# A two-layer decoder trunk on one core: six pairs of k-tiles of the last product in seven block products each

## The chip, the cores and the metric

The kernel runs on one core of a Trainium2 chip. The metric is the device time of one execution in microseconds (us). The engines that matter are TensorE (PE; its weight loads, PEld, run beside the matmuls), VectorE (DVE), ScalarE (ACT), GpSimd (POOL) and SyncE (SP), which issues the weight transfers. Each works through its own queue in order; semaphores tie them together. TensorE writes to PSUM, which has eight banks of 128 x 512 numbers of 32 bits; everything else lies in SBUF.

## The reference

Two decoder layers over 256 tokens of width 1024: the first with differential attention, the second with block-sparse attention (one block here, so causal attention), both with cross attention into a memory of 256 rows, each followed by an MLP. Only the last MLP matters here:

```python
def _sq_relu_mlp(h, w_up, w_down):
    u = jax.nn.relu(h @ w_up)
    return (u * u) @ w_down
...
x = x + _sq_relu_mlp(_rmsnorm(x, b_norm_mlp[j]), b_w_up[j], b_w_down[j])
return _rmsnorm(x, final_norm)
```

All in float32: `u` is 256 x 4096, `w_down` 4096 x 1024.

## The kernel before

**Precision.** A float32 product is made of three matmuls in the type `fp32r`. Each factor is split: a high part `h` is its copy cast to `fp32r` (on ACT), a low part `l` is the factor minus the high part (on DVE). Then a*b is ah*bh + al*bh + ah*bl, summed in a PSUM bank. So every chunk of weights (128 x 1024, 512 KB) takes one transfer into a raw buffer `w` (4 of them, L307), one cast into `wh` (6 of them, L330) and one subtraction into `wl` (6, L332); all of that stands in `chunk`.

**The last MLP** (`mlp_last`). First product, `mlp_up`: 16 blocks of two chunks; each chunk gives 128 columns of u, transposed, in an accumulator bank `acc` (4 banks). ACT and DVE add the bank's two halves into the buffer `u` (L779, L781), then relu with the row's norm factor (L787, DVE), square (L790, ACT), and the split of u into `B` tiles (L791 cast, L793 subtraction), which stay in SBUF as the left factor of the second product.

Second product: the 32 k-tiles of 128, one chunk of `w_down` each. The output 256 x 1024 is four cells of 128 x 512 (row half hf, column half c), one bank of class `t` each. For k-tiles 0 to 25, `mm` issues for each cell the three matmuls (L861) with 128 x 128 of u as the stationary and 128 x 512 of the chunk as the moving operand. The last six k-tiles (`HELD`) are kept in the six `wh`/`wl` buffers and done cell by cell, so that a cell's residual addition (L893), square sums (L895), gain (L903) and final norm run while the next cell is computed; the last cell is done in two halves, the second in a bank `acc`.

**What sets the order.** Nothing is issued as written: `P.add` records each step with its engine, an estimated time, what it reads and writes and a priority (its place, moved ahead by the numbers in `EARLY`), and `Plan.order` makes an order by list scheduling before the kernel is emitted. A step gets its buffer there: the free one with the lowest number. Buffers of class `w`, `wh`, `wl` and `acc` are handed out in the order of their first use.

## Time and profile before

| | us |
|---|---|
| median of 3 runs | 606.75 |
| the runs | 605.34, 606.75, 984.32 |
| the profiled execution | 606.42 |
| its span, first to last instruction | 604.6 |
| TensorE, DVE, ACT busy in the span | 592.3, 438.6, 377.2 |

The run of 984.32 stands alone. Busy time adds up instructions; a matmul's end is modelled, so a busy TensorE can still be waiting inside its pipeline. The chain of work that ended last follows, from the last instruction back, what released each step; the timeline lists instructions in order of time, merged where alike, with the idle time ahead of them and what ended it; the table of stretches gives each engine's busy time and the granted TensorE clock between two times.

### The profile page before, as it was taken

To read this page: it belongs to the slowest core of one execution; us is meant where nothing else is said; L and a number is where in the kernel's file an instruction comes from. 1 tells how busy PE (TensorE), PEld (TensorE's weight loads), DVE (VectorE), ACT (ScalarE), POOL (GpSimd) and SP (SyncE) were. 2 spreads that over 40 slices of the span, in tenths; PEclk is the share of its full clock that TensorE was granted. 3 is DMA by queue.
4 is the path that set the end of the run, shared out by engine and by line. 5 is a ranking of instruction groups with operands and counts; after the bars stand their busy time and mean duration, and the time that the engine had idled before them with its cause. 6 is when DMAs were issued, how large, how long until landed. Compare 5 with 4: busy or idle time off the path is not lost.

```text
span 604.6 us, 9476 instructions
## 1 busy us (share of the span) xinstructions
PE 592.3 (98%) x3430; PEld 505.1 (84%) x3430; DVE 438.6 (73%) x800; ACT 377.2 (62%) x771; POOL 55.6 (9%) x67
## 2 busy tenths in 40 slices
PE   8999999999999999999999999999999999999995
PEld 6778878988888888888888887889888888888884
DVE  6689997689887865656777788876888787544435
ACT  6878787576766654444665776776686666443422
POOL 0031020140000000101001123001300000000002
PEclk9989999999999999999999999999999999999998
DMA  8964733436655555555566435344565555555501
GB/s 317 335 206 149 261 108 107 156 129 206 217 201 181 201 178 197 185 186 194 180 208 237 145 105 171 109 140 147 185 226 178 197 184 194 189 185 198 191 20 69
DMA packets 29999, 108.39 MB, mean 179 GB/s; under 512 B 3328, under 2 KB 3328, under 8 KB 29696
## 3 DMA queue, kind: packets, MB, share of 16 engines
q1 hardware_dynamic: 29664, 107.26, 52.9%
q8 instruction: 27, 0.44, 0.3%
q10 hardware_dynamic: 288, 0.52, 0.2%
q14 instruction: 20, 0.16, 0.1%
HBM read 106.72 MB, written 1.05 MB: 178 GB/s over the span
## 4 chain that ended last, share of the span: by engine, by line
PE 93%; DMA 3%; DVE 2%; ACT 1%; issue 0%; SPq 0%; ACTq 0%
PE acc L805 29%; PE acc L493 19%; PE acc L809 15%; PE t L861 14%; PE acc L759 7%; DMA w<-wall 3%; PE t L580 2%; PE t L618 2%; PE t L675 1%; PE t L551 1%; DVE wl L332 1%; DVE xT L745 0%; ACT wh L330 0%; PE acc L861 0%; PE t L845 0%
## 5 line engine op out<-in xcount | busy, mean ns | idle before, releaser
L332 DVE TENSOR_TENSOR wl<-w,wh 128x512 fp32r<-128x512 f32 (+1 forms) x256 | 245.4, 979 | 116.7 <-ACT wh L330 114.3
L330 ACT CAST wh<-w 128x512 fp32r<-128x512 f32 (+1 forms) x256 | 208.8, 840 | 177.1 <-PE acc L805 90.6
L805 PE MATMUL acc<-xn,wh 128*128 128x512 f32 x512 | 131.3, 396 | 0.5 <-DVE xn L348 0.5
L805 PEld LDWEIGHTS acc<-xn,wh 128*128 128x128 f32 x512 | 91.1, 188 | 18.5 <-DVE xn L348 1.8
L493 PE MATMUL acc<-wh,xn 128*128 128x512 f32 x256 | 86.1, 401 | 0.9 <-ACT xn L346 0.9
L861 PE MATMUL t<-wh,B 128*128 128x512 f32 (+1 forms) x256 | 77.2, 384 | 0.0
L809 PEld LDWEIGHTS acc<-xn,wl 128*128 128x128 f32 x512 | 68.1, 188 | 5.6
L809 PE MATMUL acc<-xn,wl 128*128 128x256 f32 x512 | 69.1, 277 | 0.0
L805 PE MATMUL acc<-B,wh 128*128 128x512 f32 x256 | 64.1, 392 | 0.0
L493 PEld LDWEIGHTS acc<-wh,xn 128*128 128x128 f32 x256 | 48.0, 188 | 12.9 <-issue 1.5
L861 PEld LDWEIGHTS t<-wh,B 128*128 128x128 f32 x256 | 47.7, 188 | 9.5
L805 PEld LDWEIGHTS acc<-B,wh 128*128 128x128 f32 x256 | 46.0, 189 | 8.2
L493 PE MATMUL acc<-wl,xn 128*128 128x512 f32 x128 | 50.4, 394 | 0.1
L759 PE MATMUL acc<-B,wh 128*128 128x256 f32 x256 | 50.5, 289 | 0.0
L861 PE MATMUL t<-wl,B 128*128 128x512 f32 (+1 forms) x128 | 49.2, 384 | 0.0
L759 PEld LDWEIGHTS acc<-B,wh 128*128 128x128 f32 x256 | 41.0, 191 | 1.0 <-issue 0.8
L446 POOL TENSOR_TENSOR sqa<-sqa,sq 128x256 f32<-128x256 f32 x21 | 20.7, 988 | 226.5 <-ACT sq L445 225.9
L809 PEld LDWEIGHTS acc<-B,wl 128*128 128x128 f32 x256 | 34.9, 190 | 2.5
L759 PE MATMUL acc<-B,wl 128*128 128x256 f32 x128 | 36.1, 282 | 0.0
L527 POOL TENSOR_TENSOR ropet<-ropes,consts 128x256 f32<-128x256 f32 (+1 forms) x28 | 25.0, 912 | 120.4 <-ACT ropes L516 98.4
L809 PE MATMUL acc<-B,wl 128*128 128x256 f32 x256 | 35.7, 282 | 0.0
L599 ACT ACTIVATE B<-t,nm 128x128 f32<-128x128 f32 (+1 forms) x64 | 27.0, 441 | 7.6 <-DVE nm L595 5.7
(179 smaller groups left out, 727.1 us busy)
## 6 DMA issues: line engine op xcount, KB each, us to landing
w<-wall SPq DMA_DIRECT2D x191, 512.0 KB, 3.3
w<-memt SPq DMA_DIRECT2D x4, 512.0 KB, 4.8
B<-xnat SPq DMA_DIRECT2D x1, 1024.0 KB, 7.8
B<-mnat SPq DMA_DIRECT2D x1, 1024.0 KB, 8.3
xT<-xa SPq DMA_DIRECT2D x1, 540.0 KB, 3.6
w<-w SPq DMA_DIRECT2D x2, 256.0 KB, 3.6
xT<-xb SPq DMA_DIRECT2D x1, 512.0 KB, 6.3
consts<-consts SPq DMA_DIRECT2D x1, 256.5 KB, 4.4
```

The source lines that it names most:

```text
L330: P.add(("act", t_act(n), lambda sl=sl: nc.scalar.copy(h.t[:, sl], w.t[:, sl])), [(w, x) for x in q], [(h, x) for x in q])
L332: P.add(("dve", t_dve(n), lambda sl=sl: nc.vector.tensor_sub(l.t[:, sl], w.t[:, sl], h.t[:, sl].bitcast(F32))), [(w, x) for x in q] + [(h, ...
L446: P.add(("pool", t_pool(S), lambda: nc.gpsimd.tensor_tensor(self.acc.t, self.acc.t, sq.t, op=OP.add)), [sq, self.acc], [self.acc])
L493: nc.tensor.matmul(pss[hf].t[:, c0:c1], a(k)[:, ts], b.t[:, o + c0:o + c1], start=(k == 0 and i == 0), stop=(k == KT - 1 and i == 2))
L527: nc.gpsimd.tensor_tensor(t.t[:, 0:nh, e:e + 32], zs.t[:, 0:nh, 32 - e:64 - e], b(sin[:, e:e + 32]), op=OP.mult)
L580: nc.tensor.matmul(sp[hd].t[:, c], qk[a].t[r, qb * 128:(qb + 1) * 128], qk[b].t[r, S:S + c.stop - c.start], start=(qb == 0 and i == 0 and ...
L599: nc.scalar.activation(p[hd].t[:, c], sp[hd].t[:, c], AF.Exp, bias=nm[hd][:, qb:qb + 1], accum_out=ss[:, hd, qb:qb + 1])
L618: nc.tensor.transpose(ps.t[:, i * 128:(i + 1) * 128], p.t[:, j * 128:(j + 1) * 128], ident)
L759: nc.tensor.matmul(o, a.t[:, ws], x(k), start=(n == 0 and m % 2 == 0 and i == 0), stop=(n == KT - 1 and i == 2), skip_group_check=True)
L805: nc.tensor.matmul(ps.t, wh.t[:, k * 128:(k + 1) * 128], x(k).rearrange("p a s -> p (a s)"), start=start and k == 0, stop=stop and k == 7, ...
L809: nc.tensor.matmul(ps.t[:, 0:S], wl.t[:, k * 128:(k + 1) * 128], x(k)[:, 0], start=False, stop=stop and k == 7, skip_group_check=True)
L861: nc.tensor.matmul(ps.t[:, c0:c1], a, b.t[:, c * 512 + c0:c * 512 + c1], start=(k == k0 and i == 0), stop=(k == 31 and i == 2), skip_group ...
```

## The change

For the second product, the pairs 1, 3, 5, 7, 9 and 11 of k-tiles (`FAST`; k = 2, 3, 6, 7, and so on to 22, 23) are computed in another way. A pair is a product of 2 x 2 blocks (row halves by k-tiles) with 2 x 2 blocks (k-tiles by column halves): 8 block products. A form of Strassen's algorithm needs 7, each still in three matmuls. With A1, A2 the first row half's blocks and A3, A4 the second's, and B1, B2 / B3, B4 those of the weights:

- sums of u, made in the first product right after the square, on DVE, into tiles that are idle by then (`ppx`, `vb`, `mv`): s0 = A3+A4, s1 = s0-A1, s2 = A1-A3, s3 = A2-s1, four instructions of 128 x 128; later their split into `xn` (ACT cast, DVE subtraction, 128 x 512 each);
- sums of the weights, on DVE into the idle `xT`: t0 = B2-B1, t1 = B4-t0, t2 = B4-B2, t3 = B3-t1, 128 x 512 each;
- four weight tiles to split in place of two: B1 (512 wide), B3 and B4 (1024), t0 and t1 (1024), t2 and t3 (1024); so a fast pair holds four of the six `wh` and `wl` buffers;
- seven products: three go straight into a cell's bank, four into the four `acc` banks, which gather over all six pairs;
- after the last fast pair, `gather` adds the four banks into the residual rows `xs` (one ACT copy, eight DVE additions, 128 x 512 each).

No transfer is added. The rest of the diff renames helpers (`product` in `mm`). The core of it:

```diff
+FAST = (1, 3, 5, 7, 9, 11)
...
+            if b in sums:
+                dst, keys = sums[b]
+
+                def blocks(u=u, dst=dst):
+                    a = [u.t[:, k, hf * 128:hf * 128 + 128] for hf in range(2) for k in range(2)]
+                    s = [dst()[:, i * 128:i * 128 + 128] for i in range(4)]
+                    nc.vector.tensor_add(s[0], a[2], a[3])
+                    nc.vector.tensor_sub(s[1], s[0], a[0])
+                    nc.vector.tensor_sub(s[2], a[0], a[2])
+                    nc.vector.tensor_sub(s[3], a[1], s[1])
+                P.add(("dve", 4 * t_dve(128) + 100, blocks), [u], keys, port=True)
...
+        more = [bank("acc") for _ in range(4)]
...
+        def fast_pair(n, j):
...
+            w = [buf("w", [128, CW]) for _ in range(2)]
+            h = [buf("wh", [128, CW], F32R) for _ in range(4)]
+            l = [buf("wl", [128, CW], F32R) for _ in range(4)]
+            for a in range(2):
+                dma(lambda a=a: w[a].t, wall[i + a], 4 * 128 * CW, w=[(w[a], 0), (w[a], 1)])
...
+            def split(x, src, keys, m=CW):
+                P.add(("act", t_act(m), lambda: nc.scalar.copy(h[x].t[:, :m], src())), keys, [h[x]])
+                P.add(("dve", t_dve(m), lambda: nc.vector.tensor_sub(l[x].t[:, :m], src(), h[x].t[:, :m].bitcast(F32))),
+                      keys + [h[x]], [l[x]], port=True)
...
+            split(0, wb(0, 0), [(w[0], 0)], 512)
+            diff(0, wb(0, 1), wb(0, 0), wk[:2])
+            split(1, lambda: w[1].t, wk[2:])
+            diff(1, wb(1, 1), lambda: t(0), wk[3:] + tk(0))
+            split(2, lambda: t(0, 2), tk(0) + tk(1))
+            diff(2, wb(1, 1), wb(0, 1), [wk[1], wk[3]])
+            diff(3, wb(1, 0), lambda: t(1), [wk[2]] + tk(1))
+            split(3, lambda: t(2, 4), tk(2) + tk(3))
...
+            for ps, a, ak, x, c, last in (
+                    (more[0], u_(2 * j, 0), k0, 0, 0, end), (pss[0, 0], u_(2 * j + 1, 0), k1, 1, 0, False),
+                    (pss[0, 1], s_(3), ks, 1, 1, False), (more[1], s_(0), ks, 2, 0, end),
+                    (more[2], s_(1), ks, 2, 1, end), (more[3], s_(2), ks, 3, 0, end),
+                    (pss[1, 0], u_(2 * j + 1, 1), k1, 3, 1, False)):
+                product(ps, a, wcol(x, c), 0, 512, last, ak + [h[x], l[x]])
+            if end:
+                gather()
...
+            P.add(("act", t_act(512, True), lambda: nc.scalar.copy(vt(), r1.t)), [r1], [v])
+            to((0, 0), lambda: r1.t, r1)
+            add(vt, vt, lambda: r6.t, [v, r6], [v])
+            to((0, 1), vt, v, True)
+            to((0, 1), lambda: r5.t, r5)
+            to((1, 1), lambda: r5.t, r5)
+            add(vt, vt, lambda: r7.t, [v, r7], [v])
+            to((1, 0), vt, v, True)
+            to((1, 1), vt, v, True)
...
         for k in range(32):
+            if k // 2 in FAST:
+                ch.append(None)
+                if k % 2:
+                    fast_pair(FAST.index(k // 2), k // 2)
+                continue
             ch.append(chunk())
```

Up to block 1 of the first product of this MLP all engines' orders are as before. **TensorE, second pair of k-tiles** (k = 2, 3). Before, the chunk of k = 3 (the one of k = 2 looks the same): the four cells' banks `t`, two matmuls with the high weights and one with the low ones each:

```order
L861 MATMUL t_5624<-wh_5562,B_892_4895 128x512 x2
L861 MATMUL t_5624<-wl_5572,B_892_4895 128x512
L861 MATMUL t_5631<-wh_5562,B_892_4895 128x512 x2
L861 MATMUL t_5631<-wl_5572,B_892_4895 128x512
L861 MATMUL t_5635<-wh_5562,B_892_4895 128x512 x2
L861 MATMUL t_5635<-wl_5572,B_892_4895 128x512
L861 MATMUL t_5643<-wh_5562,B_892_4895 128x512 x2
L861 MATMUL t_5643<-wl_5572,B_892_4895 128x512
```

Now, from the second of the seven products on (the first reads `wh_5556` into the bank `acc_5697`):

```order
L892 MATMUL t_5651<-wh_5589,B_892_4895 128x512 x2
L892 MATMUL t_5651<-wl_5600,B_892_4895 128x512
L892 MATMUL t_5658<-wh_5589,xn_67 128x512 x2
L892 MATMUL t_5658<-wl_5600,xn_67 128x512
L892 MATMUL acc_5718<-wh_5616,xn_67 128x512 x2
L892 MATMUL acc_5718<-wl_5626,xn_67 128x512
L892 MATMUL acc_5724<-wh_5616,xn_67 128x512 x2
L892 MATMUL acc_5724<-wl_5626,xn_67 128x512
L892 MATMUL acc_5732<-wh_5644,xn_67 128x512 x2
L892 MATMUL acc_5732<-wl_5656,xn_67 128x512
L892 MATMUL t_5664<-wh_5644,B_892_4895 128x512 x2
L892 MATMUL t_5664<-wl_5656,B_892_4895 128x512
```

Eight groups of three per chunk pair become seven; four of the seven read the split sums in `xn`, four tiles of weights take the place of two, and each engine's order around them goes on pair by pair.

**DVE, middle of the second product.** Before, nothing but the low parts of the chunks, one row each:

```order
L332 TENSOR_TENSOR wl_5802<-w_5738,wh_5797 128x1024
L332 TENSOR_TENSOR wl_5820<-w_5756,wh_5815 128x1024
L332 TENSOR_TENSOR wl_5838<-w_5774,wh_5833 128x1024
L332 TENSOR_TENSOR wl_5856<-w_5792,wh_5851 128x1024
L332 TENSOR_TENSOR wl_5874<-w_5810,wh_5869 128x1024
```

Now, one period of a plain pair (k = 20, 21, L336) and the fast pair behind it (L926 the sums of weights, L916 the low parts):

```order
L926 TENSOR_TENSOR xT_66<-w_5992 128x512
L336 TENSOR_TENSOR wl_6023<-w_5951,wh_6017 128x1024
L926 TENSOR_TENSOR xT_66<-w_6004,xT_66 128x512
L926 TENSOR_TENSOR xT_66<-w_6004,w_5992 128x512
L926 TENSOR_TENSOR xT_66<-w_6004,xT_66 128x512
L336 TENSOR_TENSOR wl_6049<-w_5980,wh_6037 128x1024
L916 TENSOR_TENSOR wl_6056<-w_5992,wh_6044 128x512
L916 TENSOR_TENSOR wl_6063<-w_6004,wh_6054 128x1024
L916 TENSOR_TENSOR wl_6075<-xT_66,wh_6068 128x1024
L916 TENSOR_TENSOR wl_6087<-xT_66,wh_6080 128x1024
```

The four differences stand ahead of the splits that read them, around the plain chunks' splits.

**DVE, end of the second product.** Before, the last two splits around a residual addition:

```order
L332 TENSOR_TENSOR wl_6086<-w_6026,wh_6081 128x1024
L871 TENSOR_TENSOR ql_4728<-ql_4728,t_5643 128x256
L332 TENSOR_TENSOR wl_6103<-w_6044,wh_6097 128x1024
L893 TENSOR_TENSOR qh_4709<-qh_4709,t_5624 128x256 x2
L893 TENSOR_TENSOR qh_4714<-qh_4714,t_5631 128x256 x2
```

Now, the last five splits (k = 27 to 31) among the gathering additions (L972; `qh` and `ql` are the residual rows, `u_6132` the gathered copy):

```order
L336 TENSOR_TENSOR wl_6148<-w_6085,wh_6134 128x1024
L336 TENSOR_TENSOR wl_6158<-w_6111,wh_6146 128x1024
L972 TENSOR_TENSOR u_6132<-u_6132,acc_5724 128x512
L972 TENSOR_TENSOR ql_4728<-ql_4728,acc_5718 128x512
L972 TENSOR_TENSOR qh_4714<-qh_4714,u_6132 128x512
L336 TENSOR_TENSOR wl_6181<-w_6141,wh_6169 128x1024
L336 TENSOR_TENSOR wl_6189<-w_6153,wh_6179 128x1024
L972 TENSOR_TENSOR qh_4714<-qh_4714,acc_5718 128x512
L972 TENSOR_TENSOR u_6132<-u_6132,acc_5732 128x512
L972 TENSOR_TENSOR ql_4719<-ql_4719,u_6132 128x512
L336 TENSOR_TENSOR wl_6208<-w_6163,wh_6198 128x1024
L972 TENSOR_TENSOR ql_4728<-ql_4728,u_6132 128x512
```

The addition `qh_4709<-qh_4709,acc_5697`, the first one that needs a finished bank, and behind it the splits of k = 25 and 26 stand ahead of this piece; the last split now stands behind seven of the eight additions.

## Rows read from the trace of the kernel before

**Rows 1.** The page's head: span, then busy time of each engine.

```profile
span 604.6 us, 9476 instructions
PE 592.3 (98%) x3430; PEld 505.1 (84%) x3430; DVE 438.6 (73%) x800; ACT 377.2 (62%) x771; POOL 55.6 (9%) x67
```

**Rows 2.** The chain that ended last, around the last product: start, length, work.

```profile
507.70 1.86 PE acc L805 x8
509.56 0.91 PE acc L809 x8
510.47 85.13 PE t L861 x384
595.60 2.17 PE acc L861 x18
```

**Rows 3.** Busy time by stretch (count in brackets), clock, DMA share, GB/s.

```profile
core 0: us, PE busy (x) PEld busy (x) DVE busy (x) ACT busy (x) POOL busy (x), PEclk, DMA share, GB/s
440.00:510.30 70.30, 70.30 (x409) 61.30 (x409) 57.18 (x80) 48.29 (x80) 0.00 (x0) 1.00 0.58 194
510.30:597.80 87.50, 87.46 (x404) 72.97 (x402) 40.84 (x53) 32.94 (x45) 5.04 (x7) 1.00 0.45 150
597.80:604.60 6.80, 0.00 (x0) 0.00 (x0) 2.91 (x12) 1.31 (x4) 0.00 (x0) 0.75 0.21 77
```

**Rows 4.** Timeline of TensorE, last product: start, us, line, operation, tiles.

```profile
511.01 0.61 PE L861 MATMUL t<-wh,B 128*128 128x512 f32 x2
...
547.73 0.61 PE L861 MATMUL t<-wh,B 128*128 128x512 f32 x2
```

**Rows 5.** Timeline of VectorE, the last MLP's first product (idle before in brackets).

```profile
432.39 0.48 DVE L471 TENSOR_SCALAR dg<-ident,rstd 128x128 f32<-128x128 f32 x2
...
439.72 1.29 DVE L793 TENSOR_TENSOR B<-u,B 128x512 fp32r<-128x512 f32 x2
...
502.37 1.23 DVE L332 TENSOR_TENSOR wl<-w,wh 128x1024 fp32r<-128x1024 f32 x1 [0.49 <-ACT wh L330]
503.51 0.41 DVE L781 TENSOR_TENSOR u<-u,acc 128x256 f32<-128x256 f32 x1
503.84 0.68 DVE L793 TENSOR_TENSOR B<-u,B 128x512 fp32r<-128x512 f32 x1
```

**Rows 6.** Timeline of ScalarE, end of the first and of the second product.

```profile
506.83 1.06 ACT L330 CAST wh<-w 128x1024 fp32r<-128x1024 f32 x1 [1.45 <-PE acc L805]
507.78 0.63 ACT L790 ACTIVATE u<-u 128x512 f32<-128x512 f32 x1
508.31 0.35 ACT L779 COPY u<-acc 128x256 f32<-128x256 f32 x1
508.56 0.62 ACT L791 CAST B<-u 128x512 fp32r<-128x512 f32 x1
...
581.02 1.05 ACT L330 CAST wh<-w 128x1024 fp32r<-128x1024 f32 x1 [1.67 <-PE t L861]
```

**Rows 7.** Timeline of VectorE, last product: middle and end.

```profile
552.19 1.23 DVE L332 TENSOR_TENSOR wl<-w,wh 128x1024 fp32r<-128x1024 f32 x1 [1.50 <-ACT wh L330]
...
581.25 0.42 DVE L871 TENSOR_TENSOR ql<-ql,t 128x256 f32<-128x256 f32 x1 [0.64 <-PE t L861]
582.11 1.23 DVE L332 TENSOR_TENSOR wl<-w,wh 128x1024 fp32r<-128x1024 f32 x1 [0.44 <-ACT wh L330]
585.33 0.75 DVE L893 TENSOR_TENSOR qh<-qh,t 128x256 f32<-128x256 f32 x2 [2.00 <-PE t L861]
```

**Rows 8.** SP's waits from 505; its DMA issues there; page: GB/s by slice.

```profile
SPq L307 <- DVE wl L332: 51.6, 22, 3.5
...
w<-wall SPq DMA_DIRECT2D x25, 512.0 KB, 3.2
...
GB/s 317 335 206 149 261 108 107 156 129 206 217 201 181 201 178 197 185 186 194 180 208 237 145 105 171 109 140 147 185 226 178 197 184 194 189 185 198 191 20 69
```

More of the change, by code (lines that the diff above doesn't have):

```diff
@@ L252, in part, with ppx_buf @@
         return Buf(cls, lambda slot: parent.t[:, slot, 0:width], parent)
+    def ppx_buf():
+        return Buf("ppa", lambda slot: ppx[:, slot])
     def fixed(shape, nm, dt=F32):
@@ L637, in plain_T @@
         if par is None:
-            pp = [Buf("ppa", lambda slot: ppx[:, slot]) for _ in range(2)]
+            pp = [ppx_buf() for _ in range(2)]
         else:
@@ L766, in out_proj, with mlp_up @@
                 done(m)
-    def mlp_up(st):
+    def mlp_up(st, sums=()):
         st.rstd()
@@ L849, in mlp_last @@
             xs[hf, c] = x
-        us = mlp_up(st)
+        places = [ppx_buf() for _ in range(2)]
+        sums = {}
+        for i, j in enumerate(FAST):
+            if i < 2:
+                sums[j] = (lambda b=places[i]: b.t), [places[i], ("s", j)]
+            elif i < 5:
+                sums[j] = (lambda i=i: vb.rearrange("p a b e -> p (a b e)")[:, (i - 2) * 512:(i - 1) * 512]), [
+                    ("vb", n, hf) for n in range(2) for hf in range(2)] + [("s", j)]
+            else:
+                sums[j] = (lambda: mv.rearrange("p a b e -> p (a b e)")), [("mv", 0), ("mv", 1), ("s", j)]
@@ L851, in mlp_last, with product @@
+        us = mlp_up(st, sums)
         pss = {cell: bank("t") for cell in cells}
+        more = [bank("acc") for _ in range(4)]
         ch = []
-        def mm(k, hf, c, c0=0, c1=512, ps=None, k0=0):
-            wh, wl = ch[k]
-            ps = ps or pss[hf, c]
+        begun = set()
+        def product(ps, a, b, c0, c1, stop, keys):
+            start = ps not in begun
+            begun.add(ps)
             def emit():
-                uh, ul = [us[k // 4].t[:, k % 4, i, hf * 128:(hf + 1) * 128] for i in range(2)]
-                for i, (a, b) in enumerate(((uh, wh), (ul, wh), (uh, wl))):
-                    nc.tensor.matmul(ps.t[:, c0:c1], a, b.t[:, c * 512 + c0:c * 512 + c1],
-                                     start=(k == k0 and i == 0), stop=(k == 31 and i == 2), skip_group_check=True)
-            P.add(("pe", t_mm(c1 - c0, 3), emit), ukeys(us, k) + [(wh, c), (wl, c)], [ps])
+                (ah, al), (bh, bl) = a(), b()
+                for i, (x, y) in enumerate(((ah, bh), (al, bh), (ah, bl))):
+                    nc.tensor.matmul(ps.t[:, c0:c1], x, y, start=start and i == 0, stop=stop and i == 2,
+                                     skip_group_check=True)
+            P.add(("pe", t_mm(c1 - c0, 3), emit), keys, [ps])
@@ new lines, in gather, with add, to @@
+        def gather():
+            v = buf("u", [128, 2, S])
+            vt = lambda: v.t.rearrange("p a s -> p (a s)")
+            def add(dst, a, b, r, w, port=False):
+                P.add(("dve", t_dve(512), lambda: nc.vector.tensor_add(dst(), a(), b())), r, w, port=port)
+            def to(cell, src, key, port=False):
+                x = xs[cell]
+                add(lambda: x.t, lambda: x.t, src, [(x, 0), (x, 1), key], [(x, 0), (x, 1)], port)
+            r1, r5, r6, r7 = more
+            P.add(("act", t_act(512, True), lambda: nc.scalar.copy(vt(), r1.t)), [r1], [v])
[7 more added lines that the diff above has]
+            to((1, 1), vt, v, True)
@@ L883, in mlp_last @@
                         for k in range(held, 32):
-                            mm(k, hf, c, 256 * i, 256 * i + 256, tail if i else None, held if i else 0)
+                            mm(k, hf, c, 256 * i, 256 * i + 256, tail if i else None)
                         ps = tail if i else ps
```

32 lines of the change are left out of this document (added).

## The prediction

> **What bounds the kernel now.** I read the busy shares first, then the chain of waits that ended last, then a table of stretches, then the timelines. TensorE is busy for 592.3 of 604.6 us [rows 1], but a busy share says nothing of who waits for whom; the chain does. In it the whole last product is one piece, 384 matmuls in 85.13 us, followed by 18 more in 2.17 us [rows 2]: nobody releases TensorE there. The stretches agree: from 510.3 to 597.8 TensorE is busy for 87.46 of 87.50 us at a granted clock of 1.00 (the 2.4 GHz level), while VectorE (DVE) works 40.84 and ScalarE (ACT) 32.94 [rows 3]. So in this stage a matmul less is time less, as long as DVE and ACT still deliver. The last 6.8 us hold no TensorE work at all [rows 3] and aren't touched.
>
> **Removed.** A pair of k-tiles has 8 block products of 3 matmuls; a fast pair has 7. Six pairs lose 18 matmuls of 128x512. Their pace: the row at 511.01 and the row at 547.73 are 54 products of three apart [rows 4], so 36.72 us for 162, or 0.2267 each (a matmul's own 0.39 is longer, since they overlap). Removed: 18 x 0.2267 = **4.08 us**. The new products have the same shapes and the same three passes, and each bank change after three matmuls was there before, so I keep the pace.
>
> **Added on DVE and ACT.** Costs are paces, that is, start to next start while the queue is full. DVE: 1024 wide 1.14 (502.37 to 503.51), 256 wide 0.33 (503.51 to 503.84), 512 wide 0.61 (two take 1.29, one alone 0.68) [rows 5]. A tensor subtraction 128 wide isn't in the trace; between 256 and 1024 an element costs 1.05 ns, which gives 0.20; two narrow ones of another kind took 0.48 [rows 5]. I take 0.25, with 0.20 and 0.28 (a lone 256 of 0.41 less 0.13) as ends. ACT: 1024 wide 0.95 (506.83 to 507.78), 512 wide 0.53 (507.78 to 508.31) [rows 6].
>
> *Sums of u in the first product*: four 128 wide steps in six of sixteen blocks, 1.0 us each (0.8 to 1.1). A block takes 5.54 us of TensorE (two chunks of 1.86 + 0.91 [rows 2]); DVE is busy for 57.18 of 70.30 us there [rows 3], so 1.03 us of each block is free, and every second block has no sums. Hidden. What would break it: the accumulator banks are handed out lowest number first, so every second chunk reuses one bank and its eviction has one chunk (2.77 us) to be done; behind a 1.14 us split it ends some 1.1 us ahead. Late next would be the first matmul of the next chunk.
>
> *A fast pair against a plain one.* Plain: two casts and two subtractions, 1024 wide. Fast: casts 512 + 3 x 1024 + 512 (the sums); subtractions 512 + 3 x 1024 + 512; four differences of weights, 512 wide. The order repeats a plain pair and a fast pair, for which TensorE needs 24 + 21 matmuls, 10.20 us. DVE needs 5 x 1.14 + 6 x 0.61 = 9.36, ACT 5 x 0.95 + 2 x 0.53 = 5.81. So DVE goes from half idle (1.50 us before each 1.23 us split [rows 7]) to 92%, and doesn't become the bound. Rate isn't enough; lateness matters too. I laid the DVE rows of the new order on TensorE's clock, each starting at the latest of the row before, its cast, and the TensorE read that frees its buffer. Of the six high and six low tiles a fast pair holds four; each tile replaces the one six tiles earlier (two low tiles swap), so a plain tile may be split 7.5 us before its use (10.20 - 2.72). One period, zero where its plain pair starts on TensorE: the first plain tile's buffer is free at 2.72, the next one there is cast at 3.8 and split at 4.9; three differences to 6.7; second plain split 7.9; fast splits 8.5, 9.6, 11.5 (its low buffer is read until 10.20) and 12.7; the next pair's first difference 13.3; then DVE waits for the next plain cast at 14.0. It is used from 10.20 to 19.0 in this order, so each is there 5 us early. At the start, with zero at the end of the first product, the first fast pair's tiles and sums are ready at -7.0, -4.3, -0.6, 2.2 and 2.8 and are used from 5.44 to 8.84. Its first accumulator bank is free at about 3.2, after the last eviction of the first product, and used at 5.44: 2.2 us to spare. In the second pair the splits of four pairs' sums come on top; there and later 3.8 us or more remain, growing again. Nothing on TensorE waits.
>
> *Weights.* No DMA is added, and SP's order stays. Four transfers of 512 KB per 10.20 us are 206 GB/s; the slices reach 335 [rows 8]. A raw buffer of a fast pair is held longer (until its second difference or split), but was refilled in 3.2 us after release [rows 8] and comes due 4 to 5 us after it. SP already waits on DVE for its buffers (51.6 us over 22 waits [rows 8]), so a late DVE shows there first. Cost nothing.
>
> *Gathering.* One ACT copy and eight 512 wide DVE additions stand between the splits of the last eight chunks. Here the cover is thinnest. On the same clock (five periods of 10.20, a plain pair of 5.44, a product of 0.68) the last fast pair's first product is done at 57.1; DVE waits for it (0.2 for the signal), then works through seven splits and seven additions until the last chunk's low tile: 7 x 1.14 + 7 x 0.61 = 12.25, so it is ready at 69.6. The held products begin at 66.6 (57.1 + 4.08 + 5.44), and the sixth one's third matmul is the first to read it: 66.6 + 5 x 0.68 + 0.45 = 70.5. Spare: **0.9 us**, less some tenths for additions that depend on each other. Before, the same tile was ready at 583.34 (582.11 + 1.23) [rows 7] and needed at 581.03 + 3.85 = 584.88: 1.5 us. Bounds: nothing, or, with lone durations (1.23 and 0.68) in place of paces, 13.4 us and a stall of 0.2 to 0.5. I take nothing. ACT isn't the limit: its last cast began as soon as the buffer was free (581.02 [rows 6]) and takes 1.05.
>
> *A rule against it.* In rows 5 a DVE instruction starts 0.07 to 0.09 us before the end of the one before it. The Trainium skill, "VectorE: DVE Perf Modes", section "The DRAIN you can't avoid", says that the next instruction doesn't start until the pipe is empty; the trace disagrees by that overlap. By that rule DVE would pay lone durations, 5 x 1.23 + 6 x 0.68 = 10.23 per period, as much as TensorE: no rate lost, but no lateness made good. It is the third rival below.
>
> **Sum.** The profiled execution took 606.42 us (span 604.6 and 1.8 around it): 606.42 - 4.08 = 602.3. It lies 0.3 under the median of the runs shown (606.75; the other run near it took 605.34), so I say **602.4**.
>
> **Rivals.**
> 1. *Hidden, as above*: 602.4; with the runs' own spread 601.2 to 603.4. Chance 0.74.
> 2. *The gather makes the last splits late.* Each addition on DVE that costs 0.3 us more than I took delays the last low tile by 2.1 us; stalls of 0.5 to 3 us give 603 to 605.5. For it: 0.9 us is little, and additions that read the accumulators have no 512 wide row. Against: two 256 wide ones from an accumulator took 0.75 [rows 7], as on chip memory. Chance 0.14.
> 3. *DVE pays lone durations* (the rule above): the same late tile, and the second and third fast pairs eat up to 2 us of spare; stalls of 0.5 to 2 us, 603 to 604.5. Chance 0.06.
> 4. *DVE becomes the bound, slower than before.* With x for a 512 wide step the period is 5.70 + 6x and passes 10.20 at x = 0.75. The spare of some 3 us goes first; over the five periods the gain of 4.08 is gone when the excess is (4.08 + 3) / 5 = 1.42 us, x = 0.99. At x = 1.1 the stalls are 5 x (12.30 - 10.20) - 3 = 7.5, which gives 606.42 - 4.08 + 7.5 = 609.8. No row comes near (0.61 to 0.69). Chance 0.05.
> 5. *Nothing changes, because TensorE doesn't get shorter*: a pace of 0.2373 in place of 0.2267 over the 384 matmuls that remain would eat the 4.08, and give 606.4. New waits stand ahead of most products; but plain chunks wait for both engines as well, at this pace. Chance 0.01.
>
> **Range.** The first case alone spans 601.2 to 603.4. Adding the lower part of cases 2 and 3 holds eight in ten: **601.0 to 604.8**. About 2% (12 us) is what a measurement of this kernel can tell from no change. Faster by that would need three times the matmuls removed: 0.01. Slower by that needs 16 us of stalls, x about 1.4 in case 4, or a disturbance I don't see: 0.02. Within: 0.97.
>
> **What would show it.** Of the changed kernel: 402 - 18 = 384 matmuls in the last product, TensorE without idle time from 510 on, its end near 593.7 in place of 597.8, 6.8 us behind it; DVE 85 to 95% busy between 516 and 567; the last low tile split near 580. An idle stretch of TensorE shortly before a matmul of a fast pair would speak for 4, one near 580.5 for 2 or 3. I'm wrong if the matmuls' pace changes, if a bank's eviction holds a chunk of the first product, or if the splits miss their time by more than the spare named.

## The result, and the profile after

Five executions of the changed kernel have a median of 603.47 us (602.59 to 604.52); the kernel before has 606.75 beside them. The ratio is 0.9948, with a 95% interval of 0.9923 to 0.9974: a small gain of about 0.5%, inside the 2% named ahead, 1.1 us over the 602.4 that was forecast and inside its range. The profiled execution took 604.05 us; its page begins like this (columns as in [rows 1]):

```profile
span 602.3 us, 9555 instructions
PE 588.9 (98%) x3412; PEld 502.4 (83%) x3412; DVE 474.4 (79%) x874; ACT 390.8 (65%) x790; POOL 56.0 (9%) x67
```

Against [rows 1] there are 18 matmuls less, 74 instructions more on DVE and 19 more on ACT, which is what the steps of the change add up to. The span is 2.3 us shorter. Where these 2.3 us come from is read from the chain that ended last (start, length, work), the answer to [rows 2]:

```profile
511.63 5.46 PE t L892 x24
...
521.19 6.12 PE t L892 x27
...
531.42 6.12 PE t L892 x27
...
572.33 20.54 PE t L892 x99
592.87 2.17 PE acc L892 x18
```

The last product runs from 511.63 to 595.04, 83.41 us. Before it ran from 510.47 to 597.77, 87.30 us [rows 2]. So the part that was changed is 3.89 us shorter. It began 1.16 us later, though, and 0.43 us more follow behind it (602.3 - 595.04 = 7.26 us, before 604.6 - 597.77 = 6.83): -3.89 + 1.16 + 0.43 = -2.30. Neither is the change's work that was costed. Nearly all of the 0.43 us is a stretch of VectorE ahead of its last 512 wide scaling, in which it waits for nothing that the profile shows (so `issue`; before, it idles 0.1 us there):

```profile
597.80 0.42 issue
```

It stands in the chains of both profiled executions of the change and of the kernel with the gathering behind the splits, and not in those of the other kernels below; with the eighth product and with three pairs 6.87 and 6.91 us follow the last product. So it goes with the kernel and not with the execution; what makes it isn't shown. As to the start, the chains of before and after part in the kernel's first 33 us, at the first weights:

```profile
20.02 7.87 DMA w<-wall
...
32.56 9.83 PE acc L497 x35
```

Before, the same wait took 6.72 us and the same piece of TensorE's work began at 31.74. In the kernels profiled below whose first product isn't held up, the last product begins anywhere from 509.05 to 512.13. One total of one execution therefore can't show 4 us; the length of the stage can.

The stretches (columns as in [rows 3]): the first product, the last one, and the part in which the pairs with 7 products follow one another.

```profile
440.00:510.30 70.30, 70.30 (x405) 61.17 (x405) 63.65 (x108) 48.75 (x81) 0.00 (x0) 1.00 0.58 196
510.30:593.70 83.40, 83.40 (x385) 69.54 (x384) 71.19 (x98) 46.79 (x64) 4.31 (x6) 1.00 0.45 158
516.00:567.00 51.00, 51.00 (x226) 42.12 (x225) 46.08 (x54) 30.28 (x33) 0.00 (x0) 1.00 0.58 203
```

TensorE has no idle time in any of them that the table counts, at a granted clock of 1.00. DVE is busy for 46.08 of 51.00 us in the third, 90%, where 85 to 95% was forecast. In the first product DVE's busy time rose from 57.18 [rows 3] to 63.65 us in 70.30, by the sums of u and by differences that begin early.

VectorE's rows (idle before in brackets): one block's sums of u, a fast pair's differences of weights, the largest wait for a transfer, and the end of the gathering with the last low tile.

```profile
441.47 0.28 DVE L802 TENSOR_TENSOR ppx<-u 128x128 f32<-128x128 f32 x1
441.79 0.29 DVE L803 TENSOR_TENSOR ppx<-ppx,u 128x128 f32<-128x128 f32 x1
442.00 0.28 DVE L804 TENSOR_TENSOR ppx<-u 128x128 f32<-128x128 f32 x1
442.20 0.28 DVE L805 TENSOR_TENSOR ppx<-u,ppx 128x128 f32<-128x128 f32 x1
442.41 0.68 DVE L809 TENSOR_TENSOR B<-u,B 128x512 fp32r<-128x512 f32 x1
...
537.43 0.69 DVE L926 TENSOR_TENSOR xT<-w,xT 128x512 f32<-128x512 f32 x1 [0.44 <-DMA w<-wall]
538.04 0.69 DVE L926 TENSOR_TENSOR xT<-w,w 128x512 f32<-128x512 f32 x1
538.64 0.68 DVE L926 TENSOR_TENSOR xT<-w,xT 128x512 f32<-128x512 f32 x1
...
547.00 0.69 DVE L926 TENSOR_TENSOR xT<-w 128x512 f32<-128x512 f32 x1 [2.51 <-DMA w<-wall]
...
577.66 1.23 DVE L336 TENSOR_TENSOR wl<-w,wh 128x1024 fp32r<-128x1024 f32 x1 [0.56 <-ACT wh L334]
...
578.80 0.68 DVE L972 TENSOR_TENSOR qh<-qh,acc 128x512 f32<-128x512 f32 x1
579.40 0.68 DVE L972 TENSOR_TENSOR u<-u,acc 128x512 f32<-128x512 f32 x1
580.11 0.69 DVE L972 TENSOR_TENSOR ql<-ql,u 128x512 f32<-128x512 f32 x1
580.72 1.22 DVE L336 TENSOR_TENSOR wl<-w,wh 128x1024 fp32r<-128x1024 f32 x1
```

The four sums take 0.94 us (441.47 to 442.41); the differences follow at 0.61 and 0.60 us. The additions that read the accumulators (L972) take 0.68 and are followed 0.60 us later by independent work (578.80 to 579.40), but 0.71 later (579.40 to 580.11) by one that reads what the first wrote. The last low tile ends at 581.94, where a split near 580 was forecast.

TensorE's rows, first inside a pair with 7 products, then where the last low tile is first read:

```profile
548.28 0.61 PE L892 MATMUL t<-wh,B 128*128 128x512 f32 x2
...
548.96 0.62 PE L892 MATMUL t<-wh,xn 128*128 128x512 f32 x2
...
549.65 0.62 PE L892 MATMUL acc<-wh,xn 128*128 128x512 f32 x2
...
581.46 0.39 PE L892 MATMUL t<-wl,B 128*128 128x512 f32 x1
581.68 0.62 PE L892 MATMUL t<-wh,B 128*128 128x512 f32 x2
582.14 0.40 PE L892 MATMUL t<-wl,B 128*128 128x512 f32 x1
582.38 0.63 PE L892 MATMUL t<-wh,B 128*128 128x512 f32 x2
```

A product that reads u directly takes 0.68 us (548.28 to 548.96), one that reads the sums (`xn`) 0.69. The matmul that first reads the last low tile starts at 582.14, in its place, 0.68 behind the one of its kind at 581.46. The load of its stationary factor, which goes ahead of it, doesn't:

```profile
581.23 0.19 PEld L892 LDWEIGHTS t<-wl,B 128*128 128x128 f32 x1
...
581.99 0.19 PEld L892 LDWEIGHTS t<-wl,B 128*128 128x128 f32 x1
```

These loads lie 0.68 us apart, so this one was due at 581.91. It starts 0.05 us behind the split's end at 581.94. In the second profile of the change and in the kernel with raw buffers of their own (below) the same load also starts 0.05 us behind the split, and there the profile names the split as what it waited for (0.16 and 0.31 us). So nothing was left: the tile came 0.08 us late for the load, on which the wait for it sits. TensorE lost 0.02 to 0.03 us by it, since the next product starts 0.70 behind the one before (581.68 to 582.38) instead of 0.68.

SP's waits in the last product (who waits for whom: us in total, times, longest), its transfers of weights with the median time to landing, the answers to [rows 8]:

```profile
SPq L311 <- DVE wl L336: 51.1, 14, 9.0
...
w<-wall SPq DMA_DIRECT2D x26, 512.0 KB, 3.9
```

Before, 51.6 us in 22 waits, none longer than 3.5, and 3.2 us to landing [rows 8]. The total is about the same, but SP now stands for up to 9.0 us before one buffer and then sends several transfers at once, which land later. The other engines' waits in the last product (same columns) show who meets this, and ScalarE's timeline shows one of its waits near the end:

```profile
ACT wh L334 <- PE t L892: 15.7, 11, 1.7
...
DVE xT L926 <- DMA w<-wall: 3.8, 3, 2.5
```

```profile
576.57 1.05 ACT L334 CAST wh<-w 128x1024 fp32r<-128x1024 f32 x1 [1.48 <-DMA w<-wall]
```

### The profile page after: what moved, and what is told of

Same layout as the page of the kernel before. It is cut to its first block, busy times and chain, and to the rows that moved or that the text cites. A ratio compares the mean times of both kernels' runs of the same rounds, so it can differ in the third digit from the quotient of the medians.

```text
span 602.3 us, 9555 instructions
## 1 busy us (share of the span) xinstructions
PE 588.9 (98%) x3412; PEld 502.4 (83%) x3412; DVE 474.4 (79%) x874; ACT 390.8 (65%) x790; POOL 56.0 (9%) x67
## 4 chain that ended last, share of the span: by engine, by line
PE 92%; DMA 3%; DVE 3%; ACT 1%; issue 0%; SPq 0%; DVEq 0%; ACTq 0%
PE acc L821 29%; PE acc L497 19%; PE acc L825 15%; PE t L892 11%; PE acc L763 7%; PE acc L892 3%; DMA w<-wall 2%; PE t L584 2%; PE t L622 2%; PE t L679 1%; DVE wl L336 1%; PE t L555 1%; DMA xT<-xa 1%; DVE xT L749 0%; ACT wh L334 0%
## 5 line engine op out<-in xcount | busy, mean ns | idle before, releaser
L334 ACT CAST wh<-w 128x512 fp32r<-128x512 f32 (+1 forms) x244 | 196.1, 829 | 153.1 <-PE acc L821 85.8
L336 DVE TENSOR_TENSOR wl<-w,wh 128x512 fp32r<-128x512 f32 (+1 forms) x244 | 230.5, 966 | 73.8 <-ACT wh L334 73.1
L892 PE MATMUL t<-wh,B 128*128 128x512 f32 (+1 forms) x184 | 55.2, 382 | 0.0
L892 PEld LDWEIGHTS t<-wh,B 128*128 128x128 f32 x184 | 34.1, 188 | 6.7
L892 PE MATMUL t<-wl,B 128*128 128x512 f32 (+1 forms) x92 | 35.2, 382 | 0.0
```

Of the source, the lines that this page charges most:

```text
L334: P.add(("act", t_act(n), lambda sl=sl: nc.scalar.copy(h.t[:, sl], w.t[:, sl])), [(w, x) for x in q], [(h, x) for x in q])
L336: P.add(("dve", t_dve(n), lambda sl=sl: nc.vector.tensor_sub(l.t[:, sl], w.t[:, sl], h.t[:, sl].bitcast(F32))), [(w, x) for x in q] + [(h, ...
L892: nc.tensor.matmul(ps.t[:, c0:c1], x, y, start=start and i == 0, stop=stop and i == 2, skip_group_check=True)
```

## The experiments

Each kernel's last product is measured in its profile, from its first matmul to the end of its last, and its time beside that of the kernel before on the same chip. The times are medians of 10, 5, 4 and 6 executions for the eighth product, the change, the change again and the seven pairs; the others have one. The kernel before beside them has 5 executions (606.75), 13 (606.54), 1 (604.40) and 11 (607.68). The views below have the columns told above.

| kernel | last product, us | run, us | kernel before beside it, us |
|---|---|---|---|
| before | 87.30 | 606.75 | |
| the change | 83.41 | 603.47 | 606.75 |
| an eighth product | 87.46 | 606.95 | 606.54 |
| three pairs, not six | 85.34 | 604.87 | 606.54 |
| 2 more additions in the gathering | 84.68 | 605.37 | 606.54 |
| 4 more additions | 88.01 | 605.79 | 606.54 |
| differences twice | 96.39 | 617.49 | 604.40 |
| differences three times | 110.79 | 636.92 | 604.40 |
| gathering behind the splits | 83.38 | 602.60 | 604.40 |
| raw buffers of their own | 83.61 | 603.65 | 604.40 |
| the change again | 83.41 | 601.59 | 607.68 |
| seven pairs | 82.63 | 603.43 | 607.68 |
| differences twice, own raw buffers | 92.92 | 613.44 | 607.68 |
| 4 more additions, gathering behind the splits | 83.37 | 605.09 | 607.68 |

### Is it the missing product that saves the time?

Everything of the change stays, and each pair gets an eighth product back.

```diff
-  (more[0], u_(2 * j, 0), k0, 0, 0, end), (pss[0, 0], ...
+  (more[0], u_(2 * j, 0), k0, 0, 0, False), (more[0], u_(2 * j, 0), k0, 0, 0, end), (pss[0, 0], ...
```

> Every fast pair gets an eighth product of three matmuls: the first of the seven is computed twice into its bank (the output counts it double). DVE, ACT and the weights do what they do in the changed kernel. The last product took 87.30 us before (from 510.47 to 597.77) and 83.41 in the changed kernel (511.63 to 595.04). Theory (what was bought is 18 matmuls of TensorE, all that DVE got is hidden): the 18 matmuls come back at 0.227 us each, 83.41 + 4.08 = 87.5 us for the last product, and the time is that of the kernel before within 1 us. Rival (DVE or the raw weights set the pace of the changed kernel by now, and TensorE waits for them unseen): the added matmuls fill waiting time, and the product stays between 83.4 and 86.

Its chain:

```profile
509.07 5.46 PE t L892 x24
...
594.36 2.17 PE acc L892 x18
```

509.07 to 596.53 is 87.46 us, as expected, and the time is the old one (606.95 against 606.54; ratio 1.0003, 0.9978 to 1.0027). All that the change adds costs 0.16 us of this stage. The gain is the 18 matmuls and nothing else.

The second takes half the pairs:

```diff
-FAST = (1, 3, 5, 7, 9, 11)
+FAST = (1, 5, 9)
```

> Only the pairs 1, 5 and 9 are fast. Theory (each fast pair is worth 0.68 us of TensorE less 0.03 for its slightly slower products, and the gathering costs nothing): the last product takes 87.30 - 3 x 0.65 = 85.35 us. Rival (a fixed cost comes with the first fast pair, as the gathering, or a fixed gain with the new order): a loss of some tenths to 1 us against that line, 85.6 to 86.4, or 83.4 already.

Measured 510.85 to 596.19, 85.34 us. The gain goes with the number of products left out: 1.96 us for nine matmuls, 3.89 for eighteen.

### How much was there to spare in the gathering?

Two, then four more additions of 128x512 on DVE, ahead of the last low tile:

```diff
+                for _ in range(2):
+                    nc.vector.tensor_add(ppx[:, 0], vt(), r7.t)
+                nc.vector.tensor_add(vt(), vt(), r7.t)
```

The other kernel has `range(4)`; the last of these lines stood there before.

> Two more additions, 512 wide, into an idle tile, stand on DVE among the gathering ones ahead of the last chunk's split; all else is in the same order. In the changed kernel that split ended at 581.94, and the third matmul of the sixth held product, which reads it first, was due at 578.20 + 5 x 0.68 + 0.45 = 582.05. Theory by that trace (the spare is 0.1 us): 1.22 us more on DVE stall TensorE by 1.1, the last product takes 84.5. Theory of the prediction (spare 0.9): a stall of 0.3, 83.7. Rival (the gathering is off the path by more than either): 83.4.

> As the run with two more additions, but four, 2.44 us of DVE. Spare of 0.1: a stall of 2.3 us, the last product takes 85.8. Spare of 0.9: a stall of 1.5, 84.9. Off the path: 83.4. Between the two runs the stall should grow by 1.22 if the spare is used up in the first.

With two, TensorE waits before the first matmul that reads the last low tile; the chain passes through a late transfer of weights (572.25, 4.42 us), a cast, a split and the additions before it reaches this row:

```profile
583.63 0.50 PE L892 MATMUL t<-wl,B 128*128 128x512 f32 x1 [1.01 <-DVE wl L336]
```

The last product is 84.68 us, 1.27 longer. The chain has the last split ahead of it:

```profile
582.36 1.23 DVE wl L336
```

So the last low tile is ready at 583.59, 71.64 us after the product's start at 511.95, where the change has 70.31 (581.94 - 511.63): 1.33 later. What the tile loses the product loses, but for 0.06, so the change had no spare to speak of; less the forecast 0.9, two additions of 0.7 us would have given 0.5. With four the product is 88.01 us, 4.6 us longer, and its tile is ready 73.44 us after the start (581.26 + 1.23 - 509.05), 3.1 later. The rows show the rest: the wait, and the granted clock (third figure from the end of the stretches; DMA share and GB/s stand behind it).

```profile
582.53 0.80 PE L892 MATMUL t<-wl,B 128*128 128x512 f32 x1 [2.82 <-DVE wl L336]
```

```profile
579.00:582.50 3.50, 0.71 (x4) 0.25 (x2) 3.40 (x6) 0.00 (x0) 0.00 (x0) 0.99 0.00 0
582.50:585.00 2.50, 2.47 (x6) 1.99 (x7) 1.66 (x4) 0.91 (x4) 0.45 (x1) 0.50 0.00 0
585.00:588.00 3.00, 3.00 (x13) 2.45 (x12) 0.00 (x0) 0.00 (x0) 0.97 (x2) 0.86 0.00 0
```

After 2.82 us without work TensorE ran at the 1.2 GHz level (0.50) for some 3 us before it was back at 2.4: the same last 55 matmuls took 12.36 us here and 10.83 in the kernel with two more. That is another 1.5 us, paid behind the wait.

### Does DVE become the bound where the fourth rival says?

Each difference of weights is issued twice, and three times:

```diff
-  ... lambda: nc.vector.tensor_sub(t(a), x(), y())), keys, ...
+  ... lambda: [nc.vector.tensor_sub(t(a), x(), y()) for _ in range(2)]), keys, ...
```

> Each of the four 128x512 differences of a fast pair's weights is issued twice with the same result. DVE's work in a block of 10.23 us of TensorE rises from about 8.75 us, once the sums of xn's tiles are made, by 4 x 0.61 = 2.44 us to 11.2 us. Theory (DVE is a server with 10.23 us per block, and what it does not get done is carried over from block to block until the spare is gone): an excess of about 1.0 us per block over five blocks, less some 3 to 4 us of lead, so the last product is 0 to 2 us longer than the 83.4 us of the change, the run about 604 to 606 us. Rival (DVE's lone durations of 0.69 us are what counts, and its 10% of idle time cannot be used): an excess of 1.3 to 2.3 us per block, the last product 3 to 9 us longer. Second rival (DVE's added work is hidden whatever it is): no change to 83.4 us.

> The same differences are issued three times. Theory: 8.75 + 4.88 = 13.6 us of DVE's work in a block of 10.23 us, an excess of 3.4 us over five blocks and a last one, less 3 to 4 us of lead: the last product 13 us longer than 83.4 us (11 to 17), about 616 us, with TensorE waiting on DVE in every block from the second on. Lone durations: 8.75 + 8 x 0.69 = 14.3 us or more, 16 to 20 us longer. Second rival (hidden whatever it is): 83.4 us again.

Measured: 96.39 us (512.46 to 608.85), 13.0 longer than the change, and 110.79 us (517.40 to 628.19), 27.4 longer. DVE is the bound, as the theory has it, but the price is far beyond every figure expected; the runs are 617.49 and 636.92 us. The doubled kernel's rows, one block of DVE, and TensorE's waits in the last product:

```profile
543.03 1.42 DVE L926 TENSOR_TENSOR xT<-w 128x512 f32<-128x512 f32 x2 [0.71 <-DMA w<-wall]
...
555.43 1.42 DVE L926 TENSOR_TENSOR xT<-w 128x512 f32<-128x512 f32 x2 [0.72 <-DMA w<-wall]
```

```profile
PE t L892 <- DVE wl L336: 8.0, 6, 2.1
```

```profile
594.20:597.20 3.00, 2.97 (x8) 2.33 (x9) 1.66 (x4) 0.91 (x4) 0.95 (x2) 0.62 0.00 0
```

A block is 12.40 us (543.03 to 555.43), not 11.2. Two things were missed. A repeated difference writes the tile that the one before it just wrote, and starts 0.72 us behind it (1.41 less 0.69) instead of 0.61, so four cost 2.9 instead of 2.44: 11.7 us of work. And 0.7 us per block is a wait for a transfer. TensorE's own waits make 8.0 of the 13.0 us. The other 5.0 us are busy time: the same matmuls take 88.40 us in place of 83.40, at a granted clock of 0.62 behind the last wait, for instance. Two stretches make 2.8 of them: ten matmuls behind the wait of 1.85 us took 3.76 us where 2.58 were usual behind a wait, and the last 55 took 12.45 where the kernel with two more additions had 10.83; the rest is spread over the other waits. In the kernel with three, 18.8 us are waits; its first product was held up as well, by 3.6 us.

To part the work from the transfers, the doubled differences were given raw buffers of their own (the edit is shown with the kernel that has only that, below):

> The differences issued twice and, at once, raw buffers of their own for the pairs with 7 products. Theory (of the 13.0 us that the doubled differences cost, DVE's work of 11.6 us per block explains a part, its waits of some 0.7 us per block for transfers that are no longer early another): without these waits the excess is 1.4 instead of 2.1 us per block over five blocks, less 3 us of lead, 4 us of stalls and some 2 us more at the lower clock; last product 87 to 91 us. Rival (DVE waits for transfers only because it is late anyway, and its own work sets the pace): 95 to 97 us, as with shared buffers.

```profile
542.00 1.41 DVE L926 TENSOR_TENSOR xT<-wx 128x512 f32<-128x512 f32 x2
...
553.75 1.41 DVE L926 TENSOR_TENSOR xT<-wx 128x512 f32<-128x512 f32 x2
```

```profile
PE t L892 <- DVE wl L336: 6.2, 5, 2.1
```

```profile
547.26 0.50 PE L892 MATMUL t<-wl,B 128*128 128x512 f32 x1 [1.51 <-DVE wl L336]
...
590.19 0.50 PE L892 MATMUL t<-wl,B 128*128 128x512 f32 x1 [2.09 <-DVE wl L336]
```

The block is 11.75 us, nothing but work, and the last product 92.92 us: 9.5 longer than the change, 3.5 less than with shared buffers. That lies between theory and rival. The waits for transfers were a real part of the price, about a quarter; the work of DVE is the larger one. The theory's own sum, 4 us of stalls in the blocks, came out: the first wait comes only at 547.26, and the three in the blocks make 3.9 us (1.51, 1.18 and 1.22). What it left out stands in front of the products kept for the end, where nothing was spare: 0.22 and 2.09 us. And the matmuls took 3.3 us more of busy time (86.68 against 83.40) where some 2 were expected.

### What holds the last low tile?

Two candidates: the additions that stand ahead of it on DVE, and the weights that come in bursts. First the additions go behind the last split:

```diff
-            if end:
-                gather()
...
-                P.add(("dve", t_dve(512), lambda: nc.vector.tensor_add(dst(), a(), b())), r, w, port=port)
+                P.add(("dve", t_dve(512), lambda: nc.vector.tensor_add(dst(), a(), b())), r + [(ch[31][1], 0)], w,
+                      port=port)
...
+        gather()
```

Each addition now also waits for the last low tile (`ch[31][1]`).

> DVE makes the eight additions of the gathering only behind the last split of the weights instead of among the last splits. Theory (the additions stand ahead of the last low tiles on DVE and use up their spare): the last low tile is ready 2 to 3 us earlier against its need than the 0.1 us of the change, the last product keeps its 83.4 us, and the work behind it, 9.0 us to the end of the span, grows by 0 to 1 us. Rival (the late weights alone set the last low tile, and DVE has nothing to do ahead of it): the spare stays at 0.1 to 0.5 us.

```profile
577.92 1.22 DVE L336 TENSOR_TENSOR wl<-w,wh 128x1024 fp32r<-128x1024 f32 x1 [0.97 <-ACT wh L334]
```

The last low tile is ready at 579.14, 68.94 us after the product's start at 510.20; in the change it was 70.31 (581.94 - 511.63). That is 1.4 us earlier, less than the 2 to 3 expected, since DVE now waits for casts (0.97 in this row). The load ahead of the matmul isn't held any more, and the last product is 83.38 us, 0.03 under the change; 7.22 us follow it, as in the change (7.26, not the 9.0 named ahead).

Then the additions stay and the pairs with 7 products get raw buffers of their own:

```diff
-            ... "p": 4, "z": 4, "v": 2}
+            ... "p": 4, "z": 4, "v": 2, "wx": 2}
...
-            w = [buf("w", [128, CW]) for _ in range(2)]
+            w = [buf("wx", [128, CW]) for _ in range(2)]
...
-                dma(lambda a=a: w[a].t, wall[i + a], 4 * 128 * CW, w=[(w[a], 0), (w[a], 1)])
+                dma(lambda a=a: w[a].t, wall[i + a], 4 * 128 * CW, r=[("x", 0), "rb"], w=[(w[a], 0), (w[a], 1)])
```

The last line also makes these transfers wait for two tiles of this MLP (`xT`, `rb`).

> The raw weights of the fast pairs get two buffers of their own, so that the queue's next transfer does not wait for the split of a plain pair. Theory (the queue stands behind a buffer that comes free late, up to 9.0 us, and then sends four tiles at once, which land in 3.9 us instead of 3.2): DVE's waits on transfers in the last product, 3.8 us in three places, go under 1 us, and the last low tile is ready 0.5 to 1 us before its need instead of 0.1 us; the last product keeps 83.4 us. Rival (the transfers are late because all of them share the chip's memory with others): the landing stays at 3.9 us and DVE's waits at 3 us or more.

DVE's waits for transfers are gone from the list of waits of the last product (3.8 us in three places in the change), but the last low tile didn't come earlier: 581.60, which is 70.51 us after the start. The load ahead of the matmul waits 0.31 us for it, and the last product is 83.61 us. In place of the transfers DVE's splits of plain pairs wait for casts, 5.0 us in five places (1.6 in two in the change). The theory held for the middle of the product and fell for its end. SP still stands up to 9.0 us, the transfers into the buffers of their own land after 4.3 us and the others after 3.2, and two casts at the end still wait for transfers, 1.57 and 1.59 us (1.50 and 1.48 in the change). What holds these last transfers isn't shown. ACT's waits for TensorE to free high tiles (15.7 us, 11 times, in the change) suggest that raw buffers wait for a cast which waits for a high tile; that was not tried, and the kernel before had more of these waits (40.6 us, 25 times) and no late transfers.

Last, both additions and place at once, the four additions behind the last split:

> The four more additions in the gathering, which made TensorE wait 2.8 us, and the gathering behind the last split. Theory (the additions cost only because they stand ahead of the last low tile on DVE): no wait of TensorE, last product 83.4 us, its last low tile 68.9 us after the product's start as without the four. Rival (the late weights hold the last splits, wherever the additions stand): a wait of 1 us or more, 84.5 us or more.

```profile
579.84 1.23 DVE L336 TENSOR_TENSOR wl<-w,wh 128x1024 fp32r<-128x1024 f32 x1 [0.77 <-ACT wh L334]
```

Ready at 581.07, 68.94 us after the start at 512.13, to the hundredth the figure without the four; no wait, 83.37 us of last product. The same four additions that cost 4.6 us ahead of the tile cost TensorE nothing behind it. They do lengthen what follows the product, to 7.8 us.

### The change again, and a seventh pair

```diff
-HELD = 6
-FAST = (1, 3, 5, 7, 9, 11)
+HELD = 4
+FAST = (1, 3, 5, 7, 9, 11, 13)
...
```

The seventh pair's sums of u get a tile of their own, and the gathering is placed as above.

> The change itself once more, beside the seventh pair and on the same chip. Theory: 83.4 us of last product, 3.3 us (0.5%) under the kernel before. Its start of the last product should differ by about 1 us from that of the execution profiled first, since nothing ahead of the last MLP was changed.

> A seventh pair of k-tiles is made with 7 block products, the last four k-tiles stay for the end instead of six, and the gathering stands behind the last split. Theory (a matmul less is time less as long as the splits come in time): three matmuls less, 0.68 us, so the last product takes 82.7 us against 83.4 of the change; about 0.7 us under the change measured beside it. Rival (with only four plain k-tiles behind the last such pair the last splits come late): TensorE waits 1 to 3 us before the products that were kept for the end, the last product takes 84 to 87 us, and the run is 0.5 to 3 us over the change.

The change has 83.41 us of last product again, from 510.50 on, and its last low tile is ready 70.35 us after that. Its ratio is 0.9900 here (0.9879 to 0.9921; 601.59 against 607.68) and was 0.9948 (0.9923 to 0.9974) the first time. The intervals don't overlap, with the same stage to the hundredth: the rest of the program, or the chip, moves the totals by more than the intervals say. Of the 6.1 us of the second measurement the stage explains 3.9.

Seven pairs have 82.63 us of last product, 0.78 less, a little more than the three matmuls' 0.68, and TensorE waits nowhere in it; the rival fell. But 7.69 us follow instead of 7.29, and the time is 603.43 us (600.18 to 604.82; ratio 0.9930, 0.9907 to 0.9953), which isn't under the change's 601.59. It is no better version as measured; the 0.4 us that its profile leaves are too small for these runs.

## Why the prediction was right

**Removed: right, but for 0.19 us.** 4.08 us were forecast for 18 matmuls at 0.2267, and the last product lost 3.89. The eighth product put back gives the time back, and half the pairs give half.

**The pace kept: off by 0.03 us a pair.** A plain and a fast pair take 10.23 us (521.19 to 531.42 in the chain of after), not 10.20, and six times 0.03 is nearly all of the 0.19 missing; where the last low tile isn't late (83.38 us, the gathering behind the splits) 0.16 is missing. The rows place it at the products that read the sums, 0.69 apart instead of 0.68. With the eighth product the stage is 0.16 over before, so it comes with the form and not with the count. The text had taken equal shapes for equal pace; why reading from that tile is slower isn't settled.

**Sums of u: right.** 0.94 us where 1.0 was taken (0.8 to 1.1), hidden: TensorE is busy all through the first product. The narrow subtraction that the trace of before didn't show takes 0.28; the next starts 0.20 to 0.21 behind it, or 0.32 where it reads what the one before wrote (441.47 to 441.79). 0.25 was taken, 0.20 and 0.28 were the ends.

**DVE and ACT in a block: right.** 0.60 to 0.61 us for a difference, the same for an addition from the accumulators where nothing depends on the one before, and 90% busy. So the third rival fell: DVE pays paces. By the Trainium skill, "VectorE: DVE Perf Modes", section "The DRAIN you can't avoid", each of these would start only when the one before had left the pipe; the trace disagrees for independent ones (0.60 after a 0.68), and is close to it for one that reads or overwrites what the one before wrote (0.71 and 0.72). The same section of the Trainium skill lets a next instruction that isn't held start earlier (what holds one stands in "Two Vector instructions with no wait between them"), an exception that the prediction left out; the rows of independent ones agree with that. The fourth rival's mechanism exists, and its price was set too low: it counted only the excess of work, and at x = 1.1 gave 7.5 us of stalls. The doubled differences, 2.9 us more per block or x = 1.1, did make TensorE wait 8.0 us, a part of it for transfers that were early before, but they cost 13.0: the matmuls behind the waits took 5.0 us longer, partly at a lower clock, and the rival had no term for that.

**Weights at nothing: nearly right for the time, wrong in its working.** The step looked at rate and at one buffer's refill in 3.2 us. It did not follow SP's order: one queue serves plain and fast pairs, so one buffer that comes free late holds the next pair's transfers too. SP's longest wait went from 3.5 to 9.0 us, the landing from 3.2 to 3.9, and DVE waited 3.8 us for transfers. In the blocks it cost nothing, because the splits were early enough. At the end it took more than half of the forecast spare, as follows.

**Gathering: the outcome nearly right, the spare not.** 0.9 us was forecast, as 70.5 less 69.6 from the start of the product, and neither figure was right. Ready was 70.31. Of the 0.71 us by which the tile came later than laid out, 0.56 is DVE waiting for a cast (577.66) that had itself stood 1.48 us without its weights, and 0.11 is the addition that depends on the one before it (0.71 for 0.60), for which some tenths had been set aside; the sum also took the last split at its pace of 1.14, where its reader waits for all of its 1.22. Needed was not 70.5 but 70.23: the text took the matmul as what waits for the tile, and it is the load of the stationary factor ahead of it, due at 581.91 and started 0.05 us behind the split. So the tile was 0.08 us late, and the product lost some 0.03. That nothing worse came of it is partly luck: in the kernel with two more additions 1.33 us more ahead of the tile cost 1.27. The second rival was the near miss: at 0.3 us more per addition, its own figure, 2.1 us more would have stood ahead of the tile, and the runs with more additions show what that costs.

**The sum.** The stage gave 3.89 of 4.08 us. The total alone would not have told the first case from the second and third: 603.47 lies just above the first one's 601.2 to 603.4 and inside the other two. It is the stage, in which no matmul waits, that speaks for the first. Of the difference between 602.4 and 603.47 the 0.19 explains the smaller part; the rest is what the program does before and behind the last product (a start 1.16 us later and 0.43 us more at the end in the profiled execution), and with 601.59 in the second measurement it fell on the other side. That the median came within 1.1 us of the forecast is therefore in part luck.

## What to carry to other kernels

Where one engine runs without a gap, work taken off it is worth its full pace, even if the others go from half idle to 90%, provided that each added step is placed on the clock of the stage and not only summed. Look for the last item in front of the bound engine, and for the instruction that really waits for it, which here is the load ahead of a matmul and not the matmul: there the order on the helper decides, and additions that nobody awaits belong behind the split that somebody does. Follow each queue in its order, since a buffer held longer by one user delays the next user's transfer, and measure the stage, because a change of half a per cent drowns in what the rest of the program does.

## What the hardware showed unexpectedly

A wait of TensorE can cost more than its length. After 2.82 us of waiting the granted clock was 0.50 (1.2 GHz) in the next 2.5 us and 0.86 in the 3 us behind them, 1.5 us lost. After 1.01 us it stayed at 1.00. In between the length alone doesn't tell: in the kernel with doubled differences a wait of 2.10 us was followed by full clock and waits of 1.85 and 1.78 by 0.69 and 0.62 over 3 us. And in these rows DVE overlaps the end of one instruction with the next by 0.08 us where the next doesn't need or overwrite its result, and not where it does (0.60 against 0.71 and 0.72 for 128x512). Whether the engine holds it or a semaphore that the program sets isn't told apart.
